# Start addresses of the activation and weight-part buffers: slots 32 bytes longer

## The chip, the core and the metric

The kernel runs on one core of a Trainium2 chip. The metric is the device time of one execution in microseconds (us). A core has a matrix engine (TensorE: PE in the profile, its weight loads apart as PEld), a vector engine (VectorE, DVE), a scalar engine (ScalarE, ACT), GpSimd (POOL) and a queue that issues most DMAs here (SyncE, SP). They share a memory of 128 partitions (SBUF); a tile is a stretch of bytes at the same address in every partition, and "where a buffer begins" means that address.

## The reference

Two layers of a decoder trunk over 256 tokens of width 2048, in fp32. Layer 0 mixes tokens with gated linear attention, layer 1 with softmax attention that forgets; each is followed by a gated MLP of width 5632 with a causal convolution over three tokens. Every sub-layer is normalised and modulated by a vector that comes from `c` through a large matrix `w_mod`.

```python
def reference(x, c, w_mod, b_mod, ...):
    cond = jax.nn.silu(c)
    for i in range(DEPTH):                       # DEPTH = 2
        mod = (cond @ w_mod[i] + b_mod[i])[:, None, :]
        sh_m, sc_m, g_m, sh_f, sc_f, g_f = jnp.split(mod, 6, axis=-1)
        h = rmsnorm(x, norm_mix[i]) * (1.0 + sc_m) + sh_m
        y = gla_mixer(h, ...) if i % 2 == 0 else fox_mixer(h, ...)
        x = x + (1.0 + g_m) * y
        h = rmsnorm(x, norm_ffn[i]) * (1.0 + sc_f) + sh_f
        x = x + (1.0 + g_f) * conv_ffn(h, ffn_w_up[i], ffn_conv_w[i], ffn_conv_b[i], ffn_w_down[i])
    return rmsnorm(x, norm_final)
```

## The kernel before

Nearly all the time goes into streamed products: a weight matrix comes from device memory in tiles of 128 rows by 1024 columns, and each tile is multiplied once with activations that stay in SBUF. To keep fp32 accuracy with the one-pass fp32r form of the matrix engine, both operands are split in a high part and the rest, and each product is three matmuls (L540 to L542: high weight with high activation, high with low, low with high).

- **Weight tiles.** `next_w` loads a tile into one of five slots of the pool `ring` (name `w`, 4096 bytes a partition), and `split_w` makes its two parts: ScalarE copies it to `wh` (L110), VectorE subtracts to get `wl` (L111). Both have four slots of 1024 fp32, 4096 bytes.
- **Activations.** The pool `big` has twelve slots of 2048 fp32, 8192 bytes. `bigt` gives such a slot to the projections, the attention operands and the MLP's `act` and `u`; `make_h` and `raw_operand` put the two parts of four rows of activations into one (names `h` and `op`: 4 rows of 256 fp32 high, then the same low). The wide loads of `w_mod` at the start (`wm`, 1 MB each), the input `xtok`, the final gain `nfb` and the output `ot` lie there too.
- **The products.** `stream_a` (L540 to L542) holds a 128x128 block of the weight in the array and streams 256 tokens of an activation past it; `stream_b` (L573 to L575) holds 128 tokens of the activation and streams 512 columns of the weight. So one operand of each matmul lies in `big` and the other in `wh` or `wl`. `narrow` (L587 to L589) does the same for a weight of 16 columns: 16 row blocks lie beside each other in one `wh` slot, and row block k starts 64 k bytes into it.
- **Beside it.** VectorE sums the products with `w_mod` into `acc` (L248), and the small work of attention, convolution and norms is fed in between the tiles (`tick`, `steps`) at paces written as numbers.

The pools are laid out one behind the other: a scratch area for DMA descriptors (16,384 bytes), constants, `ring`, `big`, `accp`, `tmp`. As every slot length is a multiple of 128 bytes, all slots of `ring`, `big`, `wh` and `wl` begin at 32 modulo 128.

Of the kernel before, what the change touches and what calls it, by code (L numbers as in the profile page):

```python
# [9 lines left out]
F32 = mybir.dt.float32  # L10
F32R = mybir.dt.float32r
# [4 lines left out]
PSUM = bass.MemoryType.PSUM  # L16

P = 128
D = 2048
T = 256  # L20
# [11 lines left out]
AHEAD = 3  # L32
# [11 lines left out]
TAIL = 3  # L44
# [14 lines left out]
CONV_PACE = 0.7  # L59
ORDERED = ("v",)  # L60
NBIG = 12


@with_exitstack
def kernel(
# [8 lines left out]
    nc = tc.nc  # L74
# [12 lines left out]
    def nm(s):  # L87
        cnt[0] += 1
        return f"{s}_{cnt[0]}"

    def bigt(shape, s="big"):
        return big.tile(shape, F32, tag="s8", name=nm(s))

    def ringt(shape, s="w"):
        return ring.tile(shape, F32, tag="w", name=nm(s))
# [9 lines left out]

    def split_w(src):
        n_ = src.shape[-1]
        hi = tmp.tile([P, 1024], F32R, tag="wh", bufs=AHEAD + 1, name=nm("wh"))[:, :n_]
        lo = tmp.tile([P, 1024], F32R, tag="wl", bufs=AHEAD + 1, name=nm("wl"))[:, :n_]
        nc.scalar.copy(out=hi, in_=src)  # L110
        order["v"] = nc.vector.tensor_tensor(out=lo, in0=src, in1=hi.bitcast(F32), op=ALU.subtract).ins  # L111
        return hi, lo
# [1 line left out]
    def misc():  # L114
        return psM.tile([P, 512], F32, tag="m" if PS[1] else "a", name=nm("pm"))

# [1 line left out]
    ident = const.tile([P, P], F32, name="ident")  # L118
    make_identity(nc, ident)
    identr = const.tile([FH, FH], F32R, name="identr")  # L120
# [8 lines left out]
    nc.vector.tensor_scalar_mul(mgla, tri, 1.0 / 16.0)  # L129
    nc.vector.memset(mgla[0:CH, CH:P], 0.0)  # L130

# [1 line left out]
    crow = ringt([P, P], "crow")  # L133
    nc.sync.dma_start(out=crow[:KT, :], in_=c.rearrange("b (r p) -> (b r) p", p=P))
    rows = ringt([P, P], "rows")
# [59 lines left out]

    bfc = const.tile([FH, 1], F32, name="bfc")

# [1 line left out]
    mod = const.tile([P, 12, KT], F32, name="mod")  # L199
    bg = deque()  # L200

# [9 lines left out]
        return es  # L211

    def mod_tasks(l, key, f0=0, fn=D, wide=False, direct=0, defer=False):
        # columns of silu(c) @ w_mod + b_mod, finished as the layer uses them;
        # the first `direct` row tiles are summed on the tensor engine, the others on the vector engine
        s = SECT[key]
        width = fn // -(-fn // 1024)
        per = 1
# [120 lines left out]
        pace["bg"] = (len(bg) + len(pending)) / float(n_halves)  # L339
        pace["acc"] = 0.0  # L340

# [1 line left out]
    def rsqrt(dst, src, scale, nn):  # L343
        v = tmp.tile([P, 16], F32, tag="rs_v", name=nm("rv"))
        t = tmp.tile([P, 16], F32, tag="rs_t", name=nm("rt"))
# [19 lines left out]
            nc.tensor.matmul(pb[:, i * P:(i + 1) * P], ones, dg, start=True, stop=True)  # L365
        return pb

# [1 line left out]
    xT = const.tile([P, KT, T], F32, name="xT")  # L369

    def load_x():
# [37 lines left out]
                                              skip_group_check=True).ins  # L409

    def token_rstd():
        # columns of -1/sqrt(mean + eps), one per token tile
        v = tmp.tile([P, 2], F32, tag="tv", name=nm("tv"))
        t = tmp.tile([P, 2], F32, tag="tt", name=nm("tt"))
        q = tmp.tile([P, 2], F32, tag="tq", name=nm("tq"))
        nc.vector.tensor_scalar(out=v, in0=ss["p"][:, :2], scalar1=0.5 / D, scalar2=0.5 * EPS,
                                op0=ALU.mult, op1=ALU.add)
        nc.vector.tensor_scalar(out=q.bitcast(I32), in0=v.bitcast(I32), scalar1=1, scalar2=None,
                                op0=ALU.logical_shift_right)
        nc.vector.tensor_scalar(out=q.bitcast(I32), in0=q.bitcast(I32), scalar1=-1.0,  # L420
                                scalar2=float(0x5F3759DF - 0x00400000), op0=ALU.mult, op1=ALU.add)
        for _ in range(3):
            for i in range(2):
                c1 = slice(i, i + 1)
                nc.vector.tensor_scalar(out=t[:, c1], in0=q[:, c1], scalar1=q[:, c1], scalar2=v[:, c1],
                                        op0=ALU.mult, op1=ALU.mult)
            for i in range(2):
                c1 = slice(i, i + 1)
                nc.vector.tensor_scalar(out=q[:, c1], in0=t[:, c1], scalar1=1.5, scalar2=q[:, c1],
                                        op0=ALU.subtract, op1=ALU.mult)  # L430
        return q
# [11 lines left out]
    def make_h(l, kind):  # L443
        rs = token_rstd()
        with tc.issue_after(order["s"]):
            while deferred:
                deferred.pop(0)()
        pb = bcast_cols([rs[:, 0:1], rs[:, 1:2]], -1.0)
        rb = tmp.tile([P, T], F32, tag="rb", bufs=1, name=nm("rb"))
        st = {}  # L450

        def make(m):
            if m % 4 == 0:
                st["t"] = big.tile([P, 2, 4, T], F32R, tag="s8", name=nm("h"))
            if m == 2:
                nc.scalar.copy(out=rb, in_=pb[:, :T])
            t = t1("hn")
            sc, sh = modcol(l, "sc_" + kind, m), modcol(l, "sh_" + kind, m)
            hi, lo = st["t"][:, 0, m % 4, :], st["t"][:, 1, m % 4, :]
            nc.vector.tensor_tensor(out=t, in0=xT[:, m, :], in1=pb[:, :T] if m < 2 else rb, op=ALU.mult)  # L460
            nc.scalar.activation(hi, t, AF.Identity, scale=sc, bias=sh)  # L461
            nc.vector.tensor_scalar(out=t, in0=t, scalar1=sc, scalar2=sh, op0=ALU.mult, op1=ALU.add)
            ins = nc.vector.tensor_tensor(out=lo, in0=t, in1=hi.bitcast(F32), op=ALU.subtract).ins  # L463
            if m == 1:
                gate["n"], gate["ins"] = AHEAD + 1, [order["a"], ins]
            return hi, lo
        return make

    def raw_operand(tiles, nk):
        st = {}  # L470

        def make(k):
            if k % 4 == 0:
                st["t"] = big.tile([P, 2, 4, T], F32R, tag="s8", name=nm("op"))
            if k % 2 == 0:
                hi, lo = st["t"][:, 0, k % 4:k % 4 + 2, :], st["t"][:, 1, k % 4:k % 4 + 2, :]
                src = tiles[k // 8][:, k % 8:k % 8 + 2, :]
                nc.scalar.copy(out=hi, in_=src)
                nc.vector.tensor_tensor(out=lo, in0=src, in1=hi.bitcast(F32), op=ALU.subtract)  # L479
            return st["t"][:, 0, k % 4, :], st["t"][:, 1, k % 4, :]  # L480
        return lazy(make, nk, 2)

# [1 line left out]
    plan = []  # L484

    def plan_stream(w, kts, cols):
# [42 lines left out]
        return [psA.tile([P, 2, T], F32, tag="a", name=nm("pa")) for _ in range(4)]  # L529

    def stream_a(kts, cols, rhs, done=None):
        # with done: the last TAIL rows are multiplied output by output, so that done(pair) can follow early
        ps = banks()
        held = []

# [75 lines left out]
    ALL = list(range(KT))  # L611

    def log_sigmoid(dst, z, e, bias=None):
        # z may be in PSUM; min(z, 0) - log(1 + exp(-|z|))
        nc.scalar.activation(e, z, AF.Abs)
        nc.scalar.activation(e, e, AF.Exp, scale=-1.0)
        nc.scalar.activation(e, e, AF.Ln, bias=1.0)
        nc.vector.scalar_tensor_tensor(out=dst, in0=z, scalar=0.0, in1=e, op0=ALU.min, op1=ALU.subtract)

# [1 line left out]
    def gla(l, h):  # L621
        parts = {}
        pieces = [("a", 6144), ("q", 0), ("k", 1024), ("v0", 2048), ("v1", 3072), ("r0", 4096), ("r1", 5120)]
# [233 lines left out]
        set_pace(N1)  # L857
        add_residual(l, "g_m", ALL, rhs)

# [1 line left out]
    def fox(l, h):  # L861
        pf = narrow(ALL, 4 * D, FH, h)
        lf = t1("lf")[:FH, :]
# [166 lines left out]
        pace["side"], pace["sacc"] = 1.0, 0.0  # L1030
        add_residual(l, "g_m", ALL, rhs)

# [1 line left out]
    def ffn(l, h, first_blocks):  # L1034
        act = [bigt([P, 8, T], "act") for _ in range((FT + 7) // 8)]

# [76 lines left out]
            cs = slice(m * P, (m + n_) * P)  # L1113
            nc.vector.tensor_tensor(out=fin["o"][tt][:, cs], in0=pt[:, :n_ * P], in1=fin["g"][:, cs], op=ALU.mult)

# [1 line left out]
    def plan_ffn(l):  # L1117
        w = ffn_w_up[l]
        groups = []
# [139 lines left out]
```

## Time and profile before

| | |
|---|---|
| time, median of 3 runs | 2565.49 us (2560.21, 2565.49, 2566.13) |
| span of the profiled execution | 2570.5 us |
| PE busy | 2515.7 us (98%) |
| DVE busy | 1912.2 us (74%) |
| ACT busy | 1280.2 us (50%) |
| moved by DMA | 638.36 MB, mean 248 GB/s |

The profiled execution is not one of the three timed runs. Its own time is known by its span alone, 2570.5 us from the first to the last instruction, which is 5.0 us above the median. A busy share of PE counts from the start of a matmul to its modelled end, and matmuls overlap, so the pitch from one start to the next says how fast PE really goes, and the busy time of one matmul does not.

### The profile page before, as it was taken

To read this page: it belongs to the slowest core of one execution; us is meant where nothing else is said; L and a number is where in the kernel's file an instruction comes from. 1 tells how busy PE (TensorE), PEld (TensorE's weight loads), DVE (VectorE), ACT (ScalarE), POOL (GpSimd) and SP (SyncE) were. 2 spreads that over 40 slices of the span, in tenths; PEclk is the share of its full clock that TensorE was granted. 3 is DMA by queue.
4 is the path that set the end of the run, shared out by engine and by line. 5 is a ranking of instruction groups with operands and counts; after the bars stand their busy time and mean duration, and the time that the engine had idled before them with its cause. 6 is when DMAs were issued, how large, how long until landed. Compare 5 with 4: busy or idle time off the path is not lost.

```text
span 2570.5 us, 47584 instructions
## 1 busy us (share of the span) xinstructions
PE 2515.7 (98%) x19242; PEld 2431.0 (95%) x19242; DVE 1912.2 (74%) x2570; ACT 1280.2 (50%) x1956; POOL 14.6 (1%) x35
## 2 busy tenths in 40 slices
PE   6999999999999999999999999999999999999998
PEld 6988899899999999999988889999999999999998
DVE  7767988876679998877587888777766667666544
ACT  2446454445555656543454555444545555565332
POOL 0000000000000000000000000000000000000000
PEclk7999999999999999999999999999999999999999
DMA  8897978798668888889489887686777767756553
GB/s 337 282 301 226 304 245 285 261 321 299 182 183 272 296 295 286 277 310 309 153 285 311 299 265 238 227 278 202 220 223 215 222 212 229 221 183 204 181 181 115
DMA packets 184313, 638.36 MB, mean 248 GB/s; under 512 B 23961, under 2 KB 24971, under 8 KB 183708
## 3 DMA queue, kind: packets, MB, share of 16 engines
q1 hardware_dynamic: 183704, 635.17, 74.9%
q8 instruction: 150, 2.46, 0.4%
q14 instruction: 71, 0.58, 0.1%
q10 hardware_dynamic: 388, 0.15, 0.0%
HBM read 633.14 MB, written 2.10 MB: 247 GB/s over the span
## 4 chain that ended last, share of the span: by engine, by line
PE 85%; DMA 7%; DVE 4%; issue 2%; ACT 1%; DVEq 0%; SPq 0%; ACTq 0%
PE pa L542 23%; PE pa L541 23%; PE pa L540 23%; DMA wm<-in_w_mod_dram 5%; PE pa L574 4%; PE pa L573 4%; PE pa L575 4%; DVE wl L111 2%; DVE acc L248 1%; DMA w<-in_ffn_w_down_dram 1%; DMA w<-in_gla_w_out_dram 1%; ACT wh L110 1%; PE pm L261 1%; DMA w<-in_gla_w_in_dram 0%; PE pm L777 0%
## 5 line engine op out<-in xcount | busy, mean ns | idle before, releaser
L110 ACT CAST wh<-w 128x1024 fp32r<-128x1024 f32 x819 | 855.1, 1047 | 1138.2 <-PE pa L541 677.6
L111 DVE TENSOR_TENSOR wl<-w,wh 128x1024 fp32r<-128x1024 f32 x819 | 995.6, 1219 | 455.7 <-ACT wh L110 444.6
L540 PE MATMUL pa<-h,wh 128*128 128x256 f32 x3584 | 1012.6, 285 | 5.6 <-ACT h L461 5.6
L542 PE MATMUL pa<-h,wl 128*128 128x256 f32 x3584 | 1015.0, 285 | 2.6 <-DVE wl L111 2.6
L541 PE MATMUL pa<-h,wh 128*128 128x256 f32 x3584 | 1015.8, 284 | 1.0 <-DVE h L463 0.9
L540 PEld LDWEIGHTS pa<-h,wh 128*128 128x128 f32 x3584 | 688.0, 193 | 6.8 <-ACT h L461 6.5
L542 PEld LDWEIGHTS pa<-h,wl 128*128 128x128 f32 x3584 | 688.8, 193 | 5.8 <-DVE wl L111 3.3
L541 PEld LDWEIGHTS pa<-h,wh 128*128 128x128 f32 x3584 | 690.1, 193 | 1.7 <-DVE h L463 1.4
L541 PE MATMUL pa<-op,wh 128*128 128x256 f32 x1920 | 540.4, 284 | 1.9 <-DVE op L479 1.9
L540 PE MATMUL pa<-op,wh 128*128 128x256 f32 x1920 | 539.6, 284 | 1.9 <-ACT wh L110 1.6
L248 DVE SCALAR_TENSOR_TENSOR acc<-wm,cT,acc 128x1024 f32<-128x1024 f32 x352 | 450.8, 1281 | 110.0 <-DMA wm<-in_w_mod_dram 109.4
L542 PE MATMUL pa<-op,wl 128*128 128x256 f32 x1920 | 530.2, 284 | 0.1
L541 PEld LDWEIGHTS pa<-op,wh 128*128 128x128 f32 x1920 | 369.3, 192 | 2.1 <-DVE op L479 2.1
L540 PEld LDWEIGHTS pa<-op,wh 128*128 128x128 f32 x1920 | 368.5, 192 | 2.5 <-ACT wh L110 2.0
L542 PEld LDWEIGHTS pa<-op,wl 128*128 128x128 f32 x1920 | 363.1, 192 | 0.7 <-DVE wl L111 0.7
L574 PE MATMUL pa<-wh,h 128*128 128x512 f32 x512 | 201.1, 393 | 0.0
L573 PE MATMUL pa<-wh,h 128*128 128x512 f32 x512 | 199.5, 393 | 0.9 <-ACT wh L110 0.9
L575 PE MATMUL pa<-wl,h 128*128 128x512 f32 x512 | 193.1, 394 | 0.0
L573 PEld LDWEIGHTS pa<-wh,h 128*128 128x128 f32 x512 | 96.6, 189 | 20.8 <-ACT wh L110 1.3
L574 PEld LDWEIGHTS pa<-wh,h 128*128 128x128 f32 x512 | 96.5, 189 | 19.8 <-issue 0.2
L575 PEld LDWEIGHTS pa<-wl,h 128*128 128x128 f32 x512 | 96.2, 189 | 19.1
L1039 ACT ACTIVATE y<-u,cw 128x256 f32<-128x256 f32 x176 | 101.6, 599 | 4.8 <-DVE act L1055 2.4
(236 smaller groups left out, 1389.9 us busy)
## 6 DMA issues: line engine op xcount, KB each, us to landing
wm<-in_w_mod_dram SPq DMA_DIRECT2D x352, 512.0 KB, 5.0
w<-in_ffn_w_up_dram SPq DMA_DIRECT2D x320, 512.0 KB, 4.3
w<-in_ffn_w_down_dram SPq DMA_DIRECT2D x176, 512.0 KB, 4.5
w<-in_fox_w_in_dram SPq DMA_DIRECT2D x128, 512.0 KB, 5.0
w<-in_gla_w_in_dram SPq DMA_DIRECT2D x96, 512.0 KB, 5.1
wm<-in_w_mod_dram SPq DMA_DIRECT2D x16, 1024.0 KB, 12.3
w<-in_gla_w_out_dram SPq DMA_DIRECT2D x32, 512.0 KB, 5.6
w<-in_ffn_w_up_dram SPq DMA_DIRECT2D x64, 256.0 KB, 3.9
```

Source lines behind the costliest of these rows:

```text
L110: nc.scalar.copy(out=hi, in_=src)
L111: order["v"] = nc.vector.tensor_tensor(out=lo, in0=src, in1=hi.bitcast(F32), op=ALU.subtract).ins
L248: nc.vector.scalar_tensor_tensor(out=st["a"], in0=wt[:, j, :], scalar=col, in1=st["a"], op0=ALU.mult, op1=ALU.add)
L261: nc.tensor.transpose(pt[:, m * P:(m + 1) * P], st["a"][:, (q0 + m) * P:(q0 + m + 1) * P], ident)
L540: nc.tensor.matmul(o, wh[:, ms], rh, start=(first and m % 2 == 0), stop=False, skip_group_check=True)
L541: nc.tensor.matmul(o, wh[:, ms], rl, start=False, stop=False, skip_group_check=True)
L542: nc.tensor.matmul(o, wl[:, ms], rh, start=False, stop=last, skip_group_check=True)
L573: nc.tensor.matmul(o, lh[:, ts_], wh[:, hs_], start=first, stop=False)
L574: nc.tensor.matmul(o, ll[:, ts_], wh[:, hs_], start=False, stop=False)
L575: nc.tensor.matmul(o, lh[:, ts_], wl[:, hs_], start=False, stop=last)
L1039: nc.scalar.activation(y, u, AF.Identity, scale=cw[:, l * 3 + 2, r:r + 1], bias=cw[:, 6 + l, r:r + 1])
```

## The change

Each slot of `big` becomes 2056 fp32 long (8224 bytes) and each slot of `wh` and `wl` 1032 fp32 (4128 bytes). The work uses the first 2048 or 1024 of them, as before. As 8224 and 4128 leave 32 over after division by 128, successive slots of a pool begin at successive steps of 32: in the built program those of `big` at 32, 64, 96, 0, 32 and so on modulo 128, those of `wh` and of `wl` at 32, 64, 96 and 0. The slots of `ring` keep 4096 bytes and stay at 32, and all other tiles keep their place modulo 128. The slots need 640 bytes more, and the scratch area for DMA descriptors that GpSimd writes goes from 16,384 to 8192 bytes; the kernel issues no DMA from GpSimd. Comment lines are dropped, so line numbers shift by up to seven.

No instruction is added, removed or moved on any engine, and every instruction has the same waits: the two built programs differ in addresses, and in nothing else.

```diff
+SLOT = 2056
     def bigt(shape, s="big"):
-        return big.tile(shape, F32, tag="s8", name=nm(s))
+        n = 1
+        for d in shape[1:]:
+            n *= d
+        t = big.tile([P, SLOT], F32, tag="s8", name=nm(s))[:, :n]
+        if len(shape) == 3:
+            t = t.rearrange("p (a b) -> p a b", b=shape[2])
+        return t
     def split_w(src):
-        hi = tmp.tile([P, 1024], F32R, tag="wh", bufs=AHEAD + 1, name=nm("wh"))[:, :n_]
-        lo = tmp.tile([P, 1024], F32R, tag="wl", bufs=AHEAD + 1, name=nm("wl"))[:, :n_]
+        hi = tmp.tile([P, 1032], F32R, tag="wh", bufs=AHEAD + 1, name=nm("wh"))[:, :n_]
+        lo = tmp.tile([P, 1032], F32R, tag="wl", bufs=AHEAD + 1, name=nm("wl"))[:, :n_]
     # make_h
-                st["t"] = big.tile([P, 2, 4, T], F32R, tag="s8", name=nm("h"))
+                st["t"] = big.tile([P, SLOT], F32R, tag="s8", name=nm("h"))[:, :2048].rearrange("p (s k t) -> p s k t", s=2, k=4)
     # raw_operand
-                st["t"] = big.tile([P, 2, 4, T], F32R, tag="s8", name=nm("op"))
+                st["t"] = big.tile([P, SLOT], F32R, tag="s8", name=nm("op"))[:, :2048].rearrange("p (s k t) -> p s k t", s=2, k=4)
     # kernel
-    nc = _bacc.Bacc("TRN2", target_bir_lowering=False, num_devices=1)
+    nc = _bacc.Bacc("TRN2", target_bir_lowering=False, num_devices=1, dynamic_dma_scratch_size=8192)
```

## Rows read from the trace of the kernel before

**Rows 1.** The page: span, busy time, and slices with PE's share and clock.

```profile
span 2570.5 us, 47584 instructions
...
PE 2515.7 (98%) x19242; PEld 2431.0 (95%) x19242; DVE 1912.2 (74%) x2570; ACT 1280.2 (50%) x1956; POOL 14.6 (1%) x35
...
PE   6999999999999999999999999999999999999998
...
PEclk7999999999999999999999999999999999999999
```

**Rows 2.** The page's chain of work that ended last, by engine and line.

```profile
PE 85%; DMA 7%; DVE 4%; issue 2%; ACT 1%; DVEq 0%; SPq 0%; ACTq 0%
PE pa L542 23%; PE pa L541 23%; PE pa L540 23%; DMA wm<-in_w_mod_dram 5%; PE pa L574 4%; PE pa L573 4%; PE pa L575 4%; DVE wl L111 2%; DVE acc L248 1%; DMA w<-in_ffn_w_down_dram 1%; DMA w<-in_gla_w_out_dram 1%; ACT wh L110 1%; PE pm L261 1%; DMA w<-in_gla_w_in_dram 0%; PE pm L777 0%
```

**Rows 3.** The page's groups: shapes, count | busy us, mean ns | idle before.

```profile
L110 ACT CAST wh<-w 128x1024 fp32r<-128x1024 f32 x819 | 855.1, 1047 | 1138.2 <-PE pa L541 677.6
L111 DVE TENSOR_TENSOR wl<-w,wh 128x1024 fp32r<-128x1024 f32 x819 | 995.6, 1219 | 455.7 <-ACT wh L110 444.6
L540 PE MATMUL pa<-h,wh 128*128 128x256 f32 x3584 | 1012.6, 285 | 5.6 <-ACT h L461 5.6
...
L541 PE MATMUL pa<-op,wh 128*128 128x256 f32 x1920 | 540.4, 284 | 1.9 <-DVE op L479 1.9
...
L574 PE MATMUL pa<-wh,h 128*128 128x512 f32 x512 | 201.1, 393 | 0.0
```

**Rows 4.** Timeline of PE in the last MLP: start us, length us.

```profile
2299.78 0.28 PE L540 MATMUL pa<-h,wh 128*128 128x256 f32 x1
...
2301.22 0.28 PE L540 MATMUL pa<-op,wh 128*128 128x256 f32 x1
```

**Rows 5.** Timeline of PE in an attention projection (`stream_b`).

```profile
1479.78 0.39 PE L574 MATMUL pa<-wh,h 128*128 128x512 f32 x1
...
1481.60 0.39 PE L573 MATMUL pa<-wh,h 128*128 128x512 f32 x1
```

**Rows 6.** Plain fp32 matmuls: timeline of scores, chain of the output's transposes (start, us).

```profile
1505.66 0.60 PE L951 MATMUL pm<-kT,qT 128*128 128x256 f32 x2
```

```profile
2433.14 0.87 PE pm L1112 x8
```

**Rows 7.** Timeline of PE in `narrow`: first matmul of successive row blocks.

```profile
88.56 0.28 PE L587 MATMUL pm<-h,wh 128*128 128x256 f32 x1
...
88.92 0.28 PE L587 MATMUL pm<-h,wh 128*128 128x256 f32 x1
...
89.27 0.28 PE L587 MATMUL pm<-h,wh 128*128 128x256 f32 x1
...
89.63 0.28 PE L587 MATMUL pm<-h,wh 128*128 128x256 f32 x1
...
89.98 0.28 PE L587 MATMUL pm<-h,wh 128*128 128x256 f32 x1
...
91.05 0.28 PE L587 MATMUL pm<-h,wh 128*128 128x256 f32 x1
```

**Rows 8.** Groups by line on DVE: two inputs, 256 elements, different starts.

```profile
L463 DVE TENSOR_TENSOR h<-hn,h 128x256 fp32r<-128x256 f32 x64 | 25.4, 417 | 0.1
...
L460 DVE TENSOR_TENSOR hn<-xT,rb 128x256 f32<-128x256 f32 x56 | 22.4, 418 | 0.0
```

**Rows 9.** Wide loads: issues (KB, us to landing), and the chain's first pieces.

```profile
wm<-in_w_mod_dram SPq DMA_DIRECT2D x16, 1024.0 KB, 12.3
```

```profile
2.23 9.40 DMA wm<-in_w_mod_dram
11.65 10.40 DMA wm<-in_w_mod_dram
```

**Rows 10.** PE's waits for `wl`: us in total, times, longest.

```profile
PE pa L542 <- DVE wl L111: 2.6, 3, 1.2
```

## Prediction

> **What bounds the kernel now.** I read the page's head first, because a change of addresses can act only through how long single instructions and transfers take. PE is busy 98% of 2570.5 us, at full share in all slices but the first and the last, and its clock stands at full speed in nearly all of them [rows 1]. The chain of work that ended last says the same from the other side: 85% of it is PE, and the six lines of the streamed products alone make 3 x 23% + 3 x 4% = 81% [rows 2]. PE's waits for a weight part come to 2.6 us in three places [rows 10]. So the kernel goes at the pitch of PE's matmuls, and the reader should look at that pitch and at nothing else first.
>
> The pitch comes from the timelines. In the last MLP the matmuls start at 2299.78 to 2301.22, thirteen starts with twelve gaps: 1.44 / 12 = 120 ns for 256 columns [rows 4]. In a projection nine starts lie between 1479.78 and 1481.60: 1.82 / 8 = 227 ns for 512 columns [rows 5]. The counts are 3 x (3584 + 1920) = 16,512 of the first kind and 3 x 512 = 1536 of the second [rows 3], 18,048 together. 16,512 x 0.120 + 1536 x 0.227 = 1981 + 349 = 2330 us of the 2570.5. The remaining 240 us are the start, other matmuls, waits for loads (DMA has 7% of the chain, some 180 us) and stretches at the lower clock.
>
> **What the change can touch.** Instructions, order and waits stay as they are. What differs is where the operands in `big`, `wh` and `wl` begin. Four things could notice: PE reading, VectorE and ScalarE reading and writing, the DMAs into and out of `big`, and the scratch area.
>
> **PE's pitch, the term that decides.** The two pitches split into a part by columns and a fixed part: (227 - 120) / 256 = 0.418 ns a column, so 256 columns take 107 ns and each matmul carries 13 ns besides. That 13 ns is what the change could reach, if it comes from moving operand and stationary operand beginning at the same place modulo 128, as all pairs do now. Plain fp32 matmuls do not have it: eight of 128 columns take 0.87 us, 109 ns each, and of two of 256 columns that take 0.60 us the second starts 0.60 - 0.38 = 0.22 us after the first (one lasts 0.38 us there), so 128 columns more cost 0.11 us and nothing is left over [rows 6]. These too read from slots at 32 (`kT` and `qT` lie in `big`). So the equal start does not by itself cost 13 ns; the fp32r form has it and the fp32 form has not.
>
> There is a place in the kernel of before where the start of the stationary operand does change from block to block. In `narrow`, row block k begins 64 k bytes into the slot, so it lies at 32 modulo 128 for even k and at 96 for odd k, while the moving operand in `h` stays at 32. The first matmuls of the blocks start at 88.56, 88.92, 89.27, 89.63 and 89.98, and the eighth's at 91.05 [rows 7]. The steps are 0.36, 0.35, 0.36 and 0.35 us for three matmuls, and from 88.56 to 91.05 it is 2.49 / 21 = 119 ns a matmul. An odd block, with different starts, goes as an even one with equal starts, to within the 0.01 us of the timeline's last digit; 13 ns a matmul would make 0.04 us a block. And the pitch in the stream is 120 ns whether or not ScalarE and VectorE write the next `wh` and `wl` at the time, with 819 such pieces of 1.05 and 1.22 us each spread over the span [rows 3]: twelve gaps in a row without one long one [rows 4]. I find no stall that a different start could take away, and none that it could bring. I take 0 ns. The ends: at best the 11 ns by which fp32r's fixed part exceeds that of fp32 (120 against 109 for the same 256 columns streamed, if a 128-column fp32 matmul counts as two passes), at worst the 0.01 us a block that rows 7 cannot exclude, 3 ns a matmul. Both are priced as rivals.
>
> [...]
>
> **VectorE and ScalarE.** The piece with most time on the chain is `wl` (L111), 2%, then `acc` (L248), 1%, and `wh` (L110), 1% [rows 2]: 4% of 2570.5 us = 103 us at most that a slower or faster piece would move. Does the start matter to them? A subtraction whose operands all lie at 32 takes 417 ns (L463) and a product of the same size with one input at 96 (`rb`) takes 418 ns (L460) [rows 8]. The difference, 1 in 417, is 0.2 us of those 103. Value 0, ends -1 and +1 us. What hides the rest is PE: `wl` costs 1.22 us of VectorE per tile [rows 3], against 24 matmuls x 0.120 = 2.88 us of PE.
>
> **DMA.** The weight loads go to `ring`, which keeps its place, so the waits for them stay. Only the loads into `big` see another start: 16 wide ones with 12.3 us each to landing, two of the input, one gain, and 8 pieces of output. On the chain stand two wide ones, 9.40 and 10.40 us [rows 9]. They have the same size and differ by 1.0 us already, so I give the two together an end of -2 and +2 us and take 0. The halved scratch serves DMAs issued by GpSimd; there are none: 0 from both sides.
>
> **Sum.** 0 + 0 + 0 = 0 on the profiled execution's 2570.5 us, which stays 2570.5, ends -3 and +3 without PE. The profiled execution lies 5.0 us above the median of the three runs, 2565.5, and the runs differ by 6 us among themselves with the very same program. The forecast for the median is 2565 us. A measurement of this kernel can tell some 0.3%, 7.7 us, from no change.
>
> **Rivals.** First, **collisions go away** (faster). Two read streams of PE that start at the same place hinder each other, and the 13 ns are that. After the change the pair starts at different places in three cases of four, and those matmuls lose 11 ns: 0.75 x 18,048 x 11 ns = 149 us, so 2565 - 149 = 2416 us; if all lose it, 2366 us. For it speaks that the fixed part has no other explanation in the trace; against it the odd blocks of `narrow` and the fp32 matmuls from the same slots. Chance 0.05. [...]
>
> Second, **unequal starts collide** (slower). Equal starts keep two streams in step, and unequal ones let them meet: 3 ns, the most that rows 7 leave open, on three matmuls in four is 0.75 x 18,048 x 3 ns = 41 us, so 2606 us. It decides from 7.7 us / 13,536 = 0.57 ns a matmul. PE has no slack, so any such cost would pass through whole. Against it speak the same blocks of `narrow`, which have unequal starts. Chance 0.05.
>
> Third, **the slots noticed by small work alone** (faster). Pieces of VectorE at other starts, or the wide loads at a start that is a multiple of 64, gain more than their ends above: the 103 us of VectorE and ScalarE and the 20 us of wide loads, at 8% each, would give 10 us, 2555 us. Nothing in the rows points there. Chance 0.03.
>
> That the change doesn't do what it says can be left aside: the slot lengths are multiples of 32 and the pools lay them end to end.
>
> **How the numbers follow.** No change that can be told: 0.87. Faster: 0.05 + 0.03 = 0.08; slower: 0.05. The range for 8 in 10 is that of the likeliest case with the ends of the small terms and the scatter of the runs: from 2560.2 - 3 = 2557 to 2566.1 + 5 = 2571. The third rival just outside it and the two large ones are the 13% left out, with a little of the first case.
>
> **What the profile after would show.** Under the forecast the twelve gaps are 120 ns and the projection's 227, whatever the slots, and the mean of L111, L110 and L248 stays within 5 ns. Under the first rival the gaps fall to 109 ns in three tiles of four and stay at 120 in the fourth; under the second they rise by some ns in the same pattern, and PE's waits stay small. A change of time with all pitches at 120 ns would have to lie in the first 90 us or in waits for loads, and would make my DMA term wrong. The forecast fails if the pitch of PE depends on where its operands begin.

## The result, and the profile after

The changed kernel takes 2548.32 us in the median of four runs (2542.58 to 2554.96), the kernel before 2563.82 us beside it (2560.21 to 2566.13). The ratio is 0.9935, with a 95% interval from 0.9919 to 0.9951: 15.5 us less, with bounds of 12.6 and 20.8 us. The prediction said 2565 us and no change; its range began at 2557. The profiled executions lie further apart than the timed runs, 2545.8 us against 2570.5.

The head of the page of the kernel after, its chain by engine, and the groups that answer to [rows 1 to 3] (line numbers are seven higher; shapes, count | busy us, mean ns | idle before):

```profile
span 2545.8 us, 47584 instructions
...
PE 2496.7 (98%) x19242; PEld 2405.8 (95%) x19242; DVE 1910.6 (75%) x2570; ACT 1281.8 (50%) x1956; POOL 13.4 (1%) x35
...
PE 87%; DMA 6%; DVE 4%; issue 1%; ACT 1%; DVEq 0%; SPq 0%; ACTq 0%
...
L117 ACT CAST wh<-w 128x1024 fp32r<-128x1024 f32 x819 | 855.5, 1047 | 1107.2 <-PE pa L548 664.3
L118 DVE TENSOR_TENSOR wl<-w,wh 128x1024 fp32r<-128x1024 f32 x819 | 995.9, 1220 | 433.4 <-ACT wh L117 423.4
L547 PE MATMUL pa<-h,wh 128*128 128x256 f32 x3584 | 1004.9, 282 | 6.3 <-ACT h L468 6.3
```

```profile
L581 PE MATMUL pa<-wh,h 128*128 128x512 f32 x512 | 203.2, 398 | 0.0
```

VectorE's and ScalarE's pieces are what they were: 1220 ns against 1219, 1047 against 1047. PE's are not. The 256-column group went from 285 to 282 ns a matmul, and the 512-column group the other way, from 393 to 398. The length of one matmul in these rows is 164 to 166 ns more than its pitch (285 against 120, 393 against 227.5, 282 against 118.2, 398 against 231.8), so the reader should take the difference and not the value; the pitch itself is read from successive starts.

PE's timeline in the last MLP, where [rows 4] was read (start us, length us; every third matmul is copied, the two between them are left out):

```profile
2300.01 0.28 PE L547 MATMUL pa<-op,wh 128*128 128x256 f32 x1
...
2300.35 0.28 PE L547 MATMUL pa<-op,wh 128*128 128x256 f32 x1
...
2300.69 0.28 PE L547 MATMUL pa<-op,wh 128*128 128x256 f32 x1
...
2301.03 0.28 PE L547 MATMUL pa<-op,wh 128*128 128x256 f32 x1
```

Three matmuls take 0.34 us here, 1.02 / 9 = 113 ns each, where it was 120 before. Another tile of the same kernel, 400 us earlier:

```profile
1904.19 0.28 PE L547 MATMUL pa<-h,wh 128*128 128x256 f32 x1
...
1904.55 0.28 PE L547 MATMUL pa<-h,wh 128*128 128x256 f32 x1
...
1904.90 0.29 PE L547 MATMUL pa<-h,wh 128*128 128x256 f32 x1
...
1905.29 0.28 PE L547 MATMUL pa<-h,wh 128*128 128x256 f32 x1
```

Here three take 0.36, 0.35 and once 0.39 us. So the pitch goes by the tile, which it did not do before. The projection that answers to [rows 5]:

```profile
1467.63 0.39 PE L581 MATMUL pa<-wh,h 128*128 128x512 f32 x1
...
1469.72 0.40 PE L581 MATMUL pa<-wh,h 128*128 128x512 f32 x1
```

Nine gaps in 2.09 us, 232 ns where it was 227. Over all starts of the two traces at full clock, the mean pitch went from 119.95 to 118.23 ns for 256 columns and from 227.54 to 231.80 for 512. With the counts of the prediction that is 16,512 x 1.72 = 28.4 us less and 1536 x 4.26 = 6.5 us more, **21.9 us less in all**. This is the gain of the change, with its sign and roughly its size: the spans of the two profiled executions differ by 24.7 us, the medians by 15.5. In those two executions the rest adds up as well. By the starts, the gaps of over 0.4 us between matmuls at full clock went from 39.4 us in all to 28.8, and the time at the lower clock (granted 0.5, with the first 28 us, before the clock's first record, counted in) from 84.0 to 92.2 us, together 2.4 us less.

What else the prediction named moves little. Of the loads on the chain [rows 9], one took 9.39 us (9.40 before) and the other 10.46 (10.40), the wide ones again 12.3 us in the median, and PE's waits for `wl` are one of 1.2 us in place of three with 2.6 [rows 10]:

```profile
2.24 9.39 DMA wm<-in_w_mod_dram
11.65 10.46 DMA wm<-in_w_mod_dram
```

```profile
wm<-in_w_mod_dram SPq DMA_DIRECT2D x16, 1024.0 KB, 12.3
```

```profile
PE pa L549 <- DVE wl L118: 1.2, 1, 1.2
```

### The profile page after: what moved, and what is told of

Same layout as the page of the kernel before. It is cut to its first block, busy times and chain, and to the rows that moved or that the text cites. A ratio compares the mean times of both kernels' runs of the same rounds, so it can differ in the third digit from the quotient of the medians.

```text
span 2545.8 us, 47584 instructions
## 1 busy us (share of the span) xinstructions
PE 2496.7 (98%) x19242; PEld 2405.8 (95%) x19242; DVE 1910.6 (75%) x2570; ACT 1281.8 (50%) x1956; POOL 13.4 (1%) x35
## 4 chain that ended last, share of the span: by engine, by line
PE 87%; DMA 6%; DVE 4%; issue 1%; ACT 1%; DVEq 0%; SPq 0%; ACTq 0%
PE pa L548 23%; PE pa L549 23%; PE pa L547 23%; PE pa L581 4%; PE pa L580 4%; PE pa L582 4%; DMA wm<-in_w_mod_dram 4%; DVE wl L118 2%; DVE acc L255 1%; DMA w<-in_gla_w_out_dram 1%; DMA w<-in_ffn_w_down_dram 1%; PE pm L268 1%; PE pm L414 1%; ACT wh L117 0%; DMA w<-in_gla_w_in_dram 0%
## 5 line engine op out<-in xcount | busy, mean ns | idle before, releaser
L117 ACT CAST wh<-w 128x1024 fp32r<-128x1024 f32 x819 | 855.5, 1047 | 1107.2 <-PE pa L548 664.3
L118 DVE TENSOR_TENSOR wl<-w,wh 128x1024 fp32r<-128x1024 f32 x819 | 995.9, 1220 | 433.4 <-ACT wh L117 423.4
L547 PEld LDWEIGHTS pa<-h,wh 128*128 128x128 f32 x3584 | 677.2, 190 | 7.5 <-ACT h L468 7.2
L549 PEld LDWEIGHTS pa<-h,wl 128*128 128x128 f32 x3584 | 676.3, 189 | 4.0 <-issue 2.3
L548 PEld LDWEIGHTS pa<-h,wh 128*128 128x128 f32 x3584 | 677.8, 189 | 0.6 <-DVE h L470 0.3
L547 PEld LDWEIGHTS pa<-op,wh 128*128 128x128 f32 x1920 | 361.2, 188 | 4.6 <-ACT wh L117 3.8
L548 PEld LDWEIGHTS pa<-op,wh 128*128 128x128 f32 x1920 | 361.5, 188 | 1.4 <-DVE op L486 1.4
L549 PEld LDWEIGHTS pa<-op,wl 128*128 128x128 f32 x1920 | 355.3, 188 | 1.2 <-DVE wl L118 1.0
## 6 DMA issues: line engine op xcount, KB each, us to landing
wm<-in_w_mod_dram SPq DMA_DIRECT2D x16, 1024.0 KB, 12.3
```

What stands on the lines that cost most here:

```text
L547: nc.tensor.matmul(o, wh[:, ms], rh, start=(first and m % 2 == 0), stop=False, skip_group_check=True)
L548: nc.tensor.matmul(o, wh[:, ms], rl, start=False, stop=False, skip_group_check=True)
L549: nc.tensor.matmul(o, wl[:, ms], rh, start=False, stop=last, skip_group_check=True)
```

## The experiments

From here on **distance** means the start of the weight part minus the start of the activation operand that it is multiplied with. In the kernel before it is a multiple of 256 bytes for every streamed matmul. In the kernel after both sides step by 32, so the distance takes every multiple of 32, tile by tile.

Four readings of the traces were open (the recorded expectations call them theories). A: the pitch depends on the distance of PE's two operands. B: the pitch depends on the writes of ScalarE and VectorE into the next `wh` and `wl`. C: it depends on where one operand lies, whatever the other does. D: PE is not the cause, but the scratch area or the transfers.

### PE alone, all distances

The kernel has no ScalarE, VectorE or transfer at work while PE runs: two activation slots (`ma`, `mb`, the second 32 bytes further modulo 256) and sixteen pairs of weight parts (`sa` to `sp`), with 96 matmuls for each pair of slots. The slots of the weight parts are 8352 bytes long, so each begins 160 bytes further modulo 256 than the one before it, and the sixteen take every multiple of 32 modulo 512 once. In a second family the low part lies 128 bytes further than the high part, and a last one has 512 columns with the roles exchanged, as in `stream_b`.

```diff
+    for i in range(16):
+        ...
+        t = pool.tile([P, 2080 + F], F32R, tag=n, name=n)
+    ...
+            for m in range(8):
+                ...
+                nc.tensor.matmul(o, wh[:, ms], rh, ...
+                nc.tensor.matmul(o, wh[:, ms], rl, ...
+                last["mm"] = nc.tensor.matmul(o, wl[:, ms], rh, ...
```

`F` is 8, and the loop runs four times for each pair of slots, with `rh` and `rl` from `ma` or `mb` and `wh` and `wl` from one of `sa` to `sp`.

> This kernel leaves the whole trunk out: it only multiplies one activation slot (ma, and the same 32 bytes further, mb) with sixteen pairs of weight parts (sa to sp) that begin 32 bytes apart modulo 512, 96 matmuls of 256 columns for each pair, while VectorE, ScalarE and the DMAs stand still. Two families: high and low weight part beginning at the same place (lines 67 to 69), and the low part 128 bytes further (lines 80 to 82); last, 48 matmuls of 512 columns for each pair with the roles swapped (lines 97 to 99). Theory A, the two read streams of PE hinder each other by where they begin: the pitch is not one number; the pair 64 bytes apart modulo 256 (ma with sa and si) goes at 113 to 115 ns, the pair 160 apart (sh) at 120 to 121, the pair of the kernel before (256 apart, so) at exactly 120; mb gives the same numbers as ma at the same distance. Theory B, PE is hindered by what ScalarE and VectorE write into the parts: with them still, all pairs go at one and the same pitch. Theory C, only the place itself counts (a multiple of 64 or 128) and not the distance: ma and mb differ at the same distance.

Two of the groups by PE's timeline, the first matmul of each and of the group after it (start us, length us), `si` at a distance of 64 bytes modulo 256 and `so` at 0:

```profile
101.27 0.28 PE L67 MATMUL p<-ma,si 128*128 128x256 f32 x1
...
112.16 0.28 PE L67 MATMUL p<-ma,sj 128*128 128x256 f32 x1
...
168.79 0.28 PE L67 MATMUL p<-ma,so 128*128 128x256 f32 x1
...
180.31 0.28 PE L67 MATMUL p<-ma,sp 128*128 128x256 f32 x1
```

10.89 / 96 = 113.4 ns and 11.52 / 96 = 120.0 ns: the same instructions on the same data, with one operand elsewhere. Worked out likewise for all groups, ns a matmul by the distance modulo 256 (of the high part in the second row):

| distance | 0 | 32 | 64 | 96 | 128 | 160 | 192 | 224 |
|---|---|---|---|---|---|---|---|---|
| 256 columns, both parts alike | 120.0 | 118.3 | 113.3 | 118.7 | 118.6 | 120.0 | 117.8 | 116.7 |
| 256 columns, low part 128 further | 119.1 | 118.4 | 113.5 | 117.8 | 118.3 | 121.0 | 118.9 | 119.0 |
| 512 columns | 227.3 | 233.3 | 229.1 and 233.3 | 233.2 | 233.2 | 234.2 | 233.1 | 233.2 |

Distances d and d + 256 give the same (by length, `ma` with `sg` and with `so`, which lie 256 bytes apart modulo 512, 283 ns in both), and so do `ma` and `mb` at the same distance, though each operand lies elsewhere and the sums go to another slot of `psA`, the pool into which PE sums its products. (Exceptions: the first group of all, at 64, went at 117.8 once the full clock was granted, and one at 96 at 117.3; later experiments come back to these. The two of 512 columns at 64 differ too, and why was not pursued.) So the place of one operand does not matter (C falls), and the effect needs neither B nor D, since no other engine and no transfer is at work. The 120 ns of the kernel before is that of distance 0 with PE all alone.

### One half of the change at a time

The diffs here are against the kernel after. The activations' slots alone (the weight parts back to 1024):

```diff
-        hi = tmp.tile([P, 1032], F32R, tag="wh", bufs=AHEAD + 1, name=nm("wh"))[:, :n_]
-        lo = tmp.tile([P, 1032], F32R, tag="wl", bufs=AHEAD + 1, name=nm("wl"))[:, :n_]
+        hi = tmp.tile([P, 1024], F32R, tag="wh", bufs=AHEAD + 1, name=nm("wh"))[:, :n_]
+        lo = tmp.tile([P, 1024], F32R, tag="wl", bufs=AHEAD + 1, name=nm("wl"))[:, :n_]
```

> Only the slots of big are 32 bytes longer; the weight parts keep 4096 bytes. Theory A: the distance between the streams still takes all values, through the activation slot alone, and both weight parts have the same distance; from the mean pitches of the distances in the changed kernel 118 to 119 ns on average, so 16,512 x 1.5 ns = 25 us less than before and up to 7 us more at 512 columns: 2545 to 2555 us, like the whole change. Theory B: the parts lie where they lay, so no gain: 2564 us. Theory D, the gain comes from the shorter scratch or from transfers: also about 2548, but at 120 ns.

The weight parts alone:

```diff
-SLOT = 2056
+SLOT = 2048
```

> Only the slots of the weight parts are 32 bytes longer; those of big keep 8192 bytes. Theory A: each product sees one of four distances by its weight slot, whatever the activation slot: 256, 288, 320 and 352 bytes for the high part, 128 more for the low; from the changed kernel's means about 119, 118.2, 115 and 118 ns, mean 117.6, so 16,512 x 2.3 ns = 38 us less, 2525 to 2545 us, and the pitch repeats in a pattern of four weight tiles. Theory B: the whole gain too, about 2548 us. Theory D: 2548 at 120 ns.

Both sides 64 bytes further together, in the lengths of the kernel before, with half the scratch as in the kernel after:

```diff
-SLOT = 2056
+SLOT = 2048
+    padb = big.tile([P, 16], F32, tag="padb", bufs=1, name="padb")
+    nc.gpsimd.memset(padb, 0.0)
     def split_w(src):
-        hi = tmp.tile([P, 1032], F32R, tag="wh", ...
-        lo = tmp.tile([P, 1032], F32R, tag="wl", ...
+        hi = tmp.tile([P, 1024], F32R, tag="wh", ...
+        lo = tmp.tile([P, 1024], F32R, tag="wl", ...
```

> All slots have their lengths of before, and 64 bytes are left free in front of big: activations and weight parts begin at 96 modulo 128 instead of 32, at the same distance from each other as before, while the raw weights stay at 32; the scratch is halved as in the change. Theory A: the distance is that of before, so 120 and 227 ns, and 2564 us (2557 to 2571). Theory B: the writes of ScalarE and VectorE change their place against the raw weights, but not against PE: 2564 too. Theory C, the place itself counts: another pitch than 120 ns. Theory D, scratch: 2548 us.

All three were timed beside the kernel before (2566.01 us). The activations alone take 2532.33 us, ratio 0.9866 (0.9851 to 0.9881); the weight parts alone 2541.36 us, 0.9900 (0.9884 to 0.9916); both shifted together 2566.22 us, 1.0002 (0.9993 to 1.0012). The first is a miss on the good side, 13 us below the range expected: its pitch came to 117.48 ns and not to 118 to 119. From the pages, first the kernel before, then the three in their order, the group of high weight with low activation, and of the last kernel the 512 columns too:

```profile
L541 PE MATMUL pa<-h,wh 128*128 128x256 f32 x3584 | 1015.8, 284 | 1.0 <-DVE h L463 0.9
```

```profile
L548 PE MATMUL pa<-h,wh 128*128 128x256 f32 x3584 | 1004.8, 281 | 1.1 <-DVE h L470 1.0
```

```profile
L548 PE MATMUL pa<-h,wh 128*128 128x256 f32 x3584 | 1006.1, 282 | 0.2 <-DVE h L470 0.2
```

```profile
L551 PE MATMUL pa<-h,wh 128*128 128x256 f32 x3584 | 1016.5, 285 | 0.3 <-DVE h L473 0.2
...
L584 PE MATMUL pa<-wh,h 128*128 128x512 f32 x512 | 200.7, 393 | 0.0
```

Shifted together, every operand lies elsewhere and the scratch is halved, and PE goes at 285 and 393 ns beside 284 and 393 in the kernel before, pitch 119.95 and 227.54: time and pitch do not notice. Either half by itself brings a gain, and each a larger one than both together. That speaks for the distance once more: one side stepping runs through the distances in another mix than both sides stepping. Scratch and place are out as causes.

### A fixed distance

If the distance is the cause, it need not rotate. Both parts 64 bytes away, by 16 floats in front of the first `wh` (`SLOT` 2048 and parts of 1024 as before the change):

```diff
+        if "pw" not in order:
+            order["pw"] = tmp.tile([P, 16], F32, tag="padw", bufs=1, name="padw")
+            nc.gpsimd.memset(order["pw"], 0.0)
```

> Slots have their lengths of before, scratch halved; 64 bytes are left free ahead of the weight parts, so that every stationary part begins 64 bytes (modulo 256) behind the moving activations in all 16,512 matmuls of 256 columns; in the 512-column products the moving part lies 64 behind the stationary activations. Theory A, with the pitches of PE alone (113.3 ns at 64 against 120.0 at 0, and 229 to 233 against 227.3 at 512 columns): 16,512 x 6.6 = 109 us less and 3 to 9 us more; up to 20 us of the gain may go into waits for loads and for VectorE in the early stages: 2460 to 2485 us. Theory C' (it is a change of distances from product to product that helps, as in the changed kernel, and not one good distance): a constant distance gives 120 ns again, 2566 us.

The worst distance of the first experiment, 160 for the high part and 32 for the low one (40 floats in front of `wh`, and 32 in front of `wl`):

```diff
+            order["pw"] = tmp.tile([P, 40], F32, tag="padw", bufs=1, name="padw")
+            order["pl"] = tmp.tile([P, 32], F32, tag="padl", bufs=1, name="padl")
```

> The same with 160 bytes ahead of the high parts and 128 more ahead of the low ones: distances 160 (high) and 32 (low) modulo 256 everywhere. Theory A, with the pitches of PE alone (121.0 ns for that pair, 233 to 234 at 512 columns): 16,512 x 1.05 = 17 us more and 1536 x 6 = 9 us more than before, 2592 us (2580 to 2600): a kernel that differs by addresses alone and is slower. Theory C': 2566 us or less. If any departure from equal places helps: 2540.

And 64 where the weight part is stationary, 0 in `stream_b`, where the first experiment found 0 best for 512 columns:

```diff
+APART = 16
-    def split_w(src):
+    def split_w(src, off):
+        hi = tmp.tile([P, 1088], F32R, tag="wh", bufs=AHEAD + 1, name=nm("wh"))[:, off:off + n_]
+        lo = tmp.tile([P, 1088], F32R, tag="wl", bufs=AHEAD + 1, name=nm("wl"))[:, off:off + n_]
+                raws.append((wt[:, :o], 0 if ... and turned else APART))
```

> Slots of big as before; slots of the weight parts 256 bytes longer, so that they all begin at the same place modulo 256, and a tile that is used as stationary operand is written 64 bytes into its slot, one that is used as moving operand (512 columns) at its beginning: distance 64 for all products of 256 columns and 0 for all of 512. Theory A: 109 us less and nothing lost at 512 columns: 2455 to 2480 us, 3 to 9 us under the kernel with 64 bytes everywhere. Theory C': 2566.

Beside 2567.30 us for the kernel before, the first takes 2504.66 us, ratio 0.9759 (0.9722 to 0.9796), and the third 2504.09 us, 0.9755 (0.9738 to 0.9772). These are 63 us less, four times what the change brought. Both are misses none the less: 2460 to 2485 and 2455 to 2480 us were expected. Of the 109 us that 113.3 ns would save, the pitches, 115.31 and 115.25 ns, give 74 and 78, and some of that does not reach the end. That `stream_b` is at its best in the third shows in its pitch, 227.49 against 229.24 ns, which is 1536 x 1.75 = 2.7 us; the times can't tell that apart.

The second is a **miss**: it was to be slower, and takes 2569.98 us, 1.0007 (0.9993 to 1.0021), no change. Its 512 columns are as slow as foreseen, 232.73 ns, which costs 8.0 us. But the 256 columns go at 119.39 in the mean and not at the 121.0 that the same pair of distances had with PE alone. The mean hides two pitches. Two windows of that kernel (us, PE busy and how many matmuls, weight loads, VectorE, ScalarE, GpSimd, granted clock, DMA share, GB/s); a window counts all matmuls that touch it, so the pitch is its length and 0.28 us more by the count:

```profile
2100.00:2150.00 50.00, 50.00 (x416) 50.00 (x415) 32.32 (x38) 26.90 (x39) 0.00 (x0) 1.00 0.69 212
2300.00:2350.00 50.00, 50.00 (x427) 50.00 (x426) 39.07 (x54) 30.20 (x42) 0.00 (x0) 1.00 0.63 206
```

50.28 / 416 = 120.9 and 50.28 / 427 = 117.8 ns. Over all starts about half of the stream goes at 121 and half at 118: the slow half is the one foreseen, and that the time comes out where the kernel before has it is chance.

It is the same at 64. Two windows of the kernel with both parts 64 away:

```profile
700.00:750.00 50.00, 50.00 (x443) 50.00 (x443) 40.71 (x59) 30.46 (x41) 0.00 (x0) 1.00 0.65 194
2200.00:2250.00 50.00, 50.00 (x427) 50.00 (x426) 34.10 (x47) 28.30 (x40) 0.00 (x0) 1.00 0.55 180
```

At full clock and without a pause in both, 50.28 / 443 = 113.5 ns in the one and 50.28 / 427 = 117.8 ns in the other, with one and the same distance. Either value lasts for hundreds of microseconds. The mean of 115.31 ns is a mixture of two rhythms. Hence a fifth reading, E: at one distance PE can keep to either of two pitches, by what ran before. The next kernels are on it.

### Finer distances, two rhythms, and a better kernel

Distances in steps of 16, with PE alone, and each pair of slots a second time with the pairs in the opposite order (against the first kernel with PE alone; the slots are 8224 bytes long here):

```diff
-            last["copy"] = nc.vector.tensor_copy(out=t[:, 1024:2080], in_=raw[:, :1056]).ins
-            parts.append(t)
+            last["copy"] = nc.vector.tensor_copy(out=t[:, 1024:2056], in_=raw[:, 1016:2048]).ins
+            parts.append(t[:, 4 * (i // 8):2048 + 4 * (i // 8)])
...
+    for f, sts in ((rows_equal, parts), (rows_equal, parts[::-1]), (cols_equal, parts)):
```

> Leaves the whole trunk out, like the first run with PE alone: one activation slot and sixteen pairs of equal weight parts, at 32, 64, 96, 128, 160, 192, 224, 0 (sa to sh) and 48, 80, 112, 144, 176, 208, 240, 16 bytes (si to sp) behind it modulo 256; lines 67 to 69 go through them once forward and once backward, lines 82 to 84 with 512 columns. Theory A: the pitch depends on the distance alone, so forward and backward give the same, 113.3 at 64, 120.0 at 0; 48 and 80 lie near 64 if the collision is of single accesses, or are like 32 and 96 if it is of blocks of 32 bytes. Theory E, the engine keeps a rhythm from what ran before it: 64 gives 113.3 in one direction and 117.8 in the other.

The pair `ma`, `sb` (distance 64) in the first order, and then in the opposite one, each with the first matmul after it:

```profile
20.51 0.28 PE L67 MATMUL p<-ma,sb 128*128 128x256 f32 x1
...
31.41 0.28 PE L67 MATMUL p<-ma,sc 128*128 128x256 f32 x1
...
350.53 0.28 PE L67 MATMUL p<-ma,sb 128*128 128x256 f32 x1
...
361.84 0.28 PE L67 MATMUL p<-ma,sa 128*128 128x256 f32 x1
```

10.90 / 96 = 113.5 ns and 11.31 / 96 = 117.8 ns: the same operand slots; what ran before them differs, and the slot of `psA` that takes the sums. Distance 96 has two values likewise (120.0 and 117.3), and so has 224 (117.8 and 116.7). The steps between those of 32 lie between 116.7 and 120.0 ns, none as good as 64 at its best: 118.4 at 16, 117.8 and 118.3 at 48, 118.8 at 80, 120.0 at 112 and 240.

The first experiment had 113.5 ns in all four groups with the low part 128 bytes further than a high part at 64, so at 64 and 192. The kernel with that pair, all else as in the third of the fixed distances (the diff is against that one):

```diff
-        lo = tmp.tile([P, 1088], F32R, tag="wl", bufs=AHEAD + 1, name=nm("wl"))[:, off:off + n_]
+        lo = tmp.tile([P, 1088], F32R, tag="wl", bufs=AHEAD + 1, name=nm("wl"))[:, 3 * off:3 * off + n_]
```

> As the kernel with 64 bytes for stationary tiles and 0 for moving ones, but the low weight part lies 192 bytes behind the activations (modulo 256) and the high one 64. With PE alone this pair gave 113.5 to 113.7 ns in all four of its places, while 64 for both gave 113.3 in some and 117.8 in others. Theory A2 (the distances allow a few rhythms, and equal distances of 64 allow two of them, between which a chance event decides): one rhythm is left, 113.6 ns in the whole stream, so 16,512 x 6.3 = 104 us less than before in matmuls; as the last kernel turned 4.7 ns (77 us of matmuls) into 63 us, some 85 to 95 us of the 104 reach the end: 2470 to 2485 us. If the slow rhythm has another cause (loads, clock, the neighbours), it stays at 115 ns and 2504 us.

It takes **2487.21 us** against 2567.56, ratio 0.9692 (0.9678 to 0.9705): 80.4 us less than the kernel before, 61 less than the kernel after, and 2 us above the range expected, 2470 to 2485. Its windows:

```profile
700.00:750.00 50.00, 50.00 (x444) 50.00 (x442) 41.22 (x60) 29.69 (x41) 0.00 (x0) 1.00 0.69 200
2200.00:2250.00 50.00, 50.00 (x443) 50.00 (x442) 37.98 (x55) 33.52 (x49) 0.00 (x0) 1.00 0.59 190
```

443 and 444 matmuls, 113 ns, in both. The mean over all is 113.51 ns for 256 columns and 227.52 for 512. Whether the pair is what keeps the fast rhythm was tried with PE alone: twelve groups at 64 and 64, then twelve at 64 and 192, with 1 to 12 plain fp32 matmuls ahead of the next (against the first kernel with PE alone).

```diff
+    for f in (rows_equal, rows_apart):
+        for n in range(1, 13):
+            with tc.issue_after(last["mm"]):
+                banks.append(f(movs[0], parts[0], 4))
+            with tc.issue_after(last["mm"]):
+                banks.append(between(n))
```

> Leaves the whole trunk out: PE alone at a distance of 64 bytes; twelve groups of 96 matmuls with both weight parts at 64 (lines 67 to 69) and twelve with the low part at 192 (lines 80 to 82 or just behind), and after group n, n plain fp32 matmuls of 128 columns, as the kernel's modulation sums put eight of them between its tiles. Theory A2: each of the first twelve groups keeps one rhythm through its 96 matmuls, 113.3 in some and 117.8 in others; all of the second twelve go at 113.5 to 114. If the rhythm is not decided by what stands ahead, all of the first twelve are alike.

Two windows from the first family and two from the second (columns as above):

```profile
23.00:32.00 9.00, 9.00 (x82) 9.00 (x81) 0.00 (x0) 0.00 (x0) 0.00 (x0) 1.00 0.00 0
46.00:55.00 9.00, 9.00 (x78) 9.00 (x78) 0.00 (x0) 0.00 (x0) 0.00 (x0) 1.00 0.01 2
163.00:170.00 7.00, 7.00 (x64) 7.00 (x63) 0.00 (x0) 0.00 (x0) 0.00 (x0) 1.00 0.01 2
185.00:193.00 8.00, 8.00 (x73) 8.00 (x72) 0.00 (x0) 0.00 (x0) 0.00 (x0) 1.00 0.00 0
```

By the count, 9.28 / 82 = 113 and 9.28 / 78 = 119 ns in the first family, 114 and 113 in the second. By the starts, groups 2 to 12 of the first family go at 113.33 (2, 3, 6, 7, 10, 11) or 117.77 ns (4, 5, 8, 9, 12), each constant over its 96 matmuls. All twelve of the second go at 113.33 or 113.34 from their twelfth matmul on; five of them begin with some ten at up to 121. So at 64 and 192 every group fell into the fast rhythm, from whatever start. What decides at 64 and 64 is not shown. Fast and slow return every four groups, with the number of plain matmuls ahead, but so does the slot of `psA` that takes a group's sums (a group and its plain matmuls use up two of eight). Against that slot as the cause speaks that one slot took `sa` at 117.8 and `si` at 113.3 in the first experiment, and that the kernel with 64 changes it every six matmuls and keeps its pitch for hundreds of us.

### Pitch against time

The time that the pitches foretell (16,512 times the change for 256 columns and 1536 times that for 512) beside what the medians did:

| kernel | 256 columns, ns | 512 columns, ns | by the pitch, us | measured, us |
|---|---|---|---|---|
| before | 119.95 | 227.54 | | |
| after | 118.23 | 231.80 | -21.9 | -15.5 |
| activations alone | 117.48 | 232.36 | -33.4 | -33.7 |
| weight parts alone | 117.62 | 231.90 | -31.8 | -24.7 |
| both shifted together | 119.95 | 227.54 | 0 | +0.2 |
| 64 | 115.31 | 229.24 | -74.0 | -62.6 |
| 160 and 32 | 119.39 | 232.73 | -1.2 | +2.7 |
| 64, and 0 for 512 columns | 115.25 | 227.49 | -77.7 | -63.2 |
| 64 and 192, and 0 for 512 columns | 113.51 | 227.52 | -106 | -80.4 |

The pitch gives most of the size of the times and, by and large, their order. Where the gain is large, some of it doesn't arrive. The chain by engine of the two kernels at the ends, both shifted together and then 64 and 192, shows where that goes:

```profile
PE 91%; DMA 3%; DVE 3%; issue 1%; ACT 1%; SPq 0%; DVEq 0%; ACTq 0%
```

```profile
PE 81%; DMA 8%; DVE 7%; issue 2%; ACT 1%; DVEq 0%; SPq 0%; ACTq 0%
```

PE has 10 points less of the chain, and transfers and VectorE 5 and 4 more. By the starts of both traces, counted as above, the gaps of over 0.4 us between matmuls sum to 25.5 and 42.3 us, 17 us more, and time at the lower clock to 87.4 and 91.7 us, 4 more. The spans of these two executions, 2562.8 and 2477.3 us, differ by 85.5 us, 20.5 less than the 106 of the pitch, and the 21 us are that difference. (By the medians 26 us are missing; the other 5 were not traced.) Here a PE that asks for weights 5% sooner (113.51 for 119.95 ns) waits more for loads and for what VectorE makes of them: 8% and 7% of the chain, where it was 3% and 3%.

## Why the prediction was wrong, point by point

**What bounds the kernel** was right, and was what mattered: PE's pitch, 18,048 times, with little behind it that would hide a change of this size.

**The step that failed is the one on `narrow`** in the costing of PE's pitch, by which that term was put at 0; the pitches make it 21.9 us less. It took the distance modulo 128, so that blocks were "even" or "odd", and compared the one with the other. The experiments show a period of 256: with PE alone 120.0 ns at 0 and at 256 but 118.6 at 128, and 113.3 at 64 but 117.8 at 192. In `narrow` the distance runs through 0, 64, 128 and 192 from block to block, and no class of it could be compared by taking every other block. Three matmuls at one distance are also too few to show its pitch: by the trace's starts, to the nanosecond, the blocks take 358, 356, 356, 355, 355, 358 and 358 ns, and those at 64 are no faster. The signal stood in the same row, one step further: `narrow` goes at 2.49 / 21 = 119 ns [rows 7], the stream at 120 [rows 4]. With one digit more that is 118.6 against 120.0. Both numbers stood in the text, but it set only block beside block, each to 0.01 us, and called the result no difference. The 21 gaps together give the pitch to 0.5 ns and the 12 of the stream to 0.8; a window of hundreds of gaps would have made it sure. And 1.4 ns times 16,512 is 23 us, three times what the prediction called measurable. (To the nanosecond it was 2496 / 21 = 118.9 ns, so 1.1 ns and 19 us. That either comes close to the 21.9 is in part luck, as `narrow` has four of the eight distances.) The second rival even worked out that 0.57 ns a matmul decides; it then set the uncertainty at 3 ns and let the chance stand at 0.05.

**The first rival came nearest to the mechanism** (the starts of two read streams, taken together, set the pitch), with the wrong price. The runs show the dependence on the distance (113.3 to 121.0 ns); that the reads hinder each other is its explanation and was not shown. It held the effect to be all or nothing, 11 ns wherever the starts differ. In fact 6.7 of the 13 ns go, and only at the best distance (120.0 to 113.3; the 109 it counted on were reached at no distance); at most other distances it is 1 to 3 ns. The rotating slots average over all of them and reach 1.72 ns. That rival should have been several cases by size, the smallest among them the 1.4 ns of `narrow`.

**The second rival was right for 512 columns**, with about twice its 3 ns. Equal starts are best there: 227.3 against 229 to 234 ns. That they keep the two streams in step was its explanation, and was not shown either. The prediction treated both shapes as one term; the change gained 28.4 us on one and lost 6.5 on the other.

**The fp32 matmuls** [rows 6] settled nothing. By the prediction's reading they have no fixed part at their own distance (109 ns for 128 columns, 0.11 us for 128 more), which does not say that the fp32r form would keep its own at another one. In the trace of before the sixteen heads have 16 records of fp32r matmuls at L948 and 32 of plain fp32 ones at L951. The transposes that gave the 109 ns have one each (24 at L1112), so counting one as two passes was the author's estimate.

**Other engines at work.** The prediction took the pitch to be the same whether or not ScalarE and VectorE write the next parts. The runs agree: PE alone goes at 120.0 ns at distance 0, and the kernel before at 119.95.

**The small terms were right.** `wl` on VectorE, `wh` on ScalarE and the loads on the chain are the same to within 1 ns, 0 ns and 0.06 us a piece; halving the scratch costs nothing that the runs show, as the kernel shifted together has it too (1.0002). The 8% of the third rival was the author's estimate, and no piece showed it. The order of instructions is unchanged. "The forecast fails if the pitch of PE depends on where its operands begin" is what happened.

**Not settled.** The change's medians give 15.5 us where its pitches give 21.9. Its runs spread over 12 us, so that may be scatter, and it was not pursued. The kernel before had medians of 2566.0, 2567.3 and 2567.6 us in the 35 runs beside the experiments, 2 to 4 us above the four beside the change. Why the period is 256 bytes, and what puts a stretch into one rhythm or the other, was not found out either.

## What to carry to other kernels

Where PE bounds, read its pitch from starts over dozens of matmuls, and multiply a difference by the count before calling it rounding: a little over 1 ns was some 20 us here. The distance between the stationary and the moving operand is a layout parameter that cost one pad of 64 bytes, or 256 bytes a weight slot in the best kernel; try it with PE alone, for each shape, and in the order in which the kernel issues its matmuls. Look for a second pitch before you trust a mean: at 64, and at 160 and 32, half of the stream went at another. A fixed good distance (64 and 192 for 256 columns, 0 for 512) was worth five times as much as one that rotates through all.

## What the hardware showed that was not expected

The pitch of fp32r matmuls, with PE alone and at full clock, depends on the distance of its two operands modulo 256 bytes, in steps as fine as 16 (113.3 to 121.0 ns for 256 columns; 227.3 to 234.2 for 512, in steps of 32). The best distance for one shape is not that of the other: 256 columns take 113.3 ns at 64 and 120.0 at 0, 512 columns 229.1 or 233.3 at 64 and 227.3 at 0. The two shapes also differ in which operand is stationary. And at one and the same distance PE can keep to either of two pitches, 113.3 or 117.8 ns at 64, 121 or 118 at 160 and 32, for 100 us and more; what puts it into one of them was not found out.
